# A two-layer hybrid encoder trunk on one core: loads in order of need, block 1 transposed behind the first unit, zero products, and the last two units of a segment finished one PSUM bank ahead of the other

## The chip, the cores and the metric

The kernel runs on one core of one Trainium2 chip. The metric is device time in microseconds (us) of one execution; the figure for a kernel is the median of its runs.

## The reference

A sequence of 256 frames of width 1024 goes through two layers. Each layer computes, with ALPHA = (2*2)^(1/4):

```python
x = layer_norm(ALPHA * x + 0.5 * swiglu(x, ffn1_w_gu[l], ffn1_w_down[l]), ln1_g[l], ln1_b[l])
h = x @ w_in[l]                      # one input projection for three groups of heads
...                                  # differential attention | Mamba-2 SSD | gated DeltaNet
x = layer_norm(ALPHA * x + mix, ln2_g[l], ln2_b[l])      # mix = concat(heads) @ w_out[l]
x = layer_norm(ALPHA * x + 0.5 * swiglu(x, ffn2_w_gu[l], ffn2_w_down[l]), ln3_g[l], ln3_b[l])
```

`swiglu(x, gu, down)` is `(silu(gate) * up) @ down` with `gate, up` the two halves of `x @ gu`; the inner width is 2816. Everything is float32. The change touches only how the big products are fed and ordered, not the heads between `w_in` and `w_out`.

## The kernel before

**Blocks and segments.** The 256 frames are two blocks of 128 rows, b = 0 and b = 1, held in the tiles `x0` and `x1` (the order listings below call them `x_91` and `x_92`). The work is six segments: FFN 1, mix and FFN 2 of layer 0, then of layer 1. At a segment's end each block is normalised (`norm`: `x` plus the segment's output, mean and variance, gain and bias) and transposed (`make_xT`), and the next segment starts from the transposed tiles `xT`, one for each half of the 1024 columns. So there are five boundaries between segments: 0 to 1 and 3 to 4 go from FFN 1 into mix, 2 to 3 from FFN 2 into FFN 1, and 1 to 2 and 4 to 5 from mix into FFN 2.

**Units.** A segment is a list of units. A unit is one piece of weights of at most 1024 columns per partition: loaded by SP's DMA queue into a tile `raw` (`load`, 5 buffers), then split by ACT and DVE into a high part `wh` and a low part `wl` (`split`, 7 buffers each, two halves per unit). Float32 accuracy comes from three products of split operands (`mm3`, lines 217 to 228): high times high, high times low, low times high. Line 221 is xh*wh, line 222 xh*wl, lines 224 and 228 xl*wh; line 228 stands after both banks, line 224 is used on a unit that ends its sum:

```python
for p, (wh, wl) in zip(ps, ws):
    mm(p, lhsT=xh, rhs=wh, ...)          # 221
    mm(p, lhsT=xh, rhs=wl, ...)          # 222
    if stop: mm(p, lhsT=xl, rhs=wh, ...) # 224
if not stop:
    for p, (wh, wl) in zip(ps, ws): mm(p, lhsT=xl, rhs=wh, ...)  # 228
```

So a product with `xl` needs DVE's subtraction at line 233 (`xT<-xps,xT`), a product with `xh` only ACT's copy at line 232. The first two column groups of an FFN and some units of mix run one block at a time; the others ("both") run both blocks in one pass with the weights stationary (line 301). The `down` and `w_out` units at a segment's end run one block at a time into two PSUM banks `po[0]` and `po[1]`, one for each half of the output's columns.

**Which block runs when.** `order` (line 1107) lists (block, unit) pairs. In a segment's first and last phase block 0 runs ahead of block 1 by up to LAG = 5 units. At the end block 0 finishes its last unit five units before block 1 does, so block 0's norm and its transposition can run beside block 1's remaining products.

**What sets the order on the engines.** The Python program emits instructions while it advances a clock of its own (`self.clock`) by the length of each product; `norm`, `make_xT` and the like are generators that yield a number of microseconds and are taken up again by `step` once that clock has passed (`spawn`, `go`, `step`). `norm` yields 5.5 (times 0.9) before it goes on to `make_xT` (line 389). The tile framework then assigns the emitted instructions to the engines' queues; every engine works through its queue strictly in order. `norm` reads `po[0]` at its first line-375 instruction and `po[1]` at its second, takes statistics (376, 378), an inverse root on POOL (394, 396) and writes `x` in halves (382, 383).

**The start.** `setup` loads 64 KB of constants and `x0` in two halves of 256 KB, `prepare` loads five units (two DMAs of 256 KB each), then `x1` follows. `make_xT` is spawned for both blocks before the first product. In segment 0 units 0 to 3 hold the first column group, units 0 and 1 for the first half of the 1024 inputs, units 2 and 3 for the second.

Of the kernel before, what the change touches and what calls it, by code (L numbers as in the profile page):

```python
# [17 lines left out]
P = 128  # L18
# [5 lines left out]
NCH = DFF // 256  # L24
# [67 lines left out]
class Kernel:  # L92
# [47 lines left out]
    def setup(self):  # L140
        nc, a = self.nc, self.a
        c = self.const
        self.x = [c.tile([P, D], F32, name=f"x{b}") for b in range(2)]
        cst = c.tile([P, C_N], F32, name="cst")
        nc.sync.dma_start(cst[:, 0:P], a["cst"][:, 0:P])
        self.load_x(0)
        self.cst = cst
        self.ident = cst[:, C_ID : C_ID + P]
        self.UT = cst[:, C_UT : C_UT + P]
        self.SL = cst[:, C_SL : C_SL + P]  # L150
        self.M1 = cst[:, C_M1 : C_M1 + 64]
        self.ident64 = cst[:, C_I64 : C_I64 + 64]
        self.sel = cst[:, C_SEL : C_SEL + 2]
        self.neghalf = c.tile([P, 16], F32, name="neghalf")
        nc.gpsimd.memset(self.neghalf, -0.5)

    def load_x(self, b):
        for n in range(2):
            s = slice(n * 512, (n + 1) * 512)
            self.nc.sync.dma_start(self.x[b][:, s], self.a["x"][0, b * P : (b + 1) * P, s])  # L160

    def setup_late(self):

# [77 lines left out]
    def load(self, u):  # L241
        nc = self.nc
        raw = self.raw_p.tile([P, 1024], F32, tag="raw", name=self.name("raw"))
        if u["kind"] in ("gu", "win"):
            width, ks = u["width"], u["ks"]
            t = raw[:, : ks * width].rearrange("p (k n) -> p k n", k=ks)
            at = 0
            k0 = u["part"] * ks * P
            for c0, n in u["cols"]:
                nc.sync.dma_start(  # L250
                    t[:, :, at : at + n], u["w"][k0 : k0 + ks * P, c0 : c0 + n].rearrange("(k p) n -> p k n", p=P)
                )
                at += n
            u["n"] = ks * width
        else:
            nc.sync.dma_start(raw, u["w"][u["k"] * P : (u["k"] + 1) * P, :])
            u["n"] = 1024
        u["raw"] = raw
# [16 lines left out]
    def job(self, u, b):  # L275


        wh, wl = u["wh"], u["wl"]
        if u["kind"] in ("gu", "win"):
            width, ks = u["width"], u["ks"]  # L280
            g = u["group"]
            if u["part"] == 0:
                g["ps", b] = [self.ps("ps") for _ in range(2 if u["kind"] == "gu" and u["both"] else 1)]
            banks = g["ps", b]
            last = u["part"] == KD // ks - 1
            if u["both"]:
                for i, c0 in enumerate(u["tiles"]):
                    for kk in range(ks):
                        k = u["part"] * ks + kk
                        x = self.xT[k // 4][:, k % 4].rearrange("p a b t -> p a (b t)")  # L290
                        s = slice(kk * width + c0, kk * width + c0 + P)
                        end = last and kk == ks - 1
                        if len(banks) == 2:

                            o, first = banks[i][:, 0:256], k == 0
                            mms = [(banks[i], wh[:, s], x.rearrange("p a t -> p (a t)")), (o, wl[:, s], x[:, 0])]
                        else:
                            o, first = banks[0][:, 256 * i : 256 * i + 256], k == 0 and i == 0
# [12 lines left out]
            ps = banks[0][:, :width]  # L311
            for kk in range(ks):
                k = u["part"] * ks + kk
                xh, xl = (self.xT[k // 4][:, k % 4, part, b, :] for part in range(2))
                s = slice(kk * width, (kk + 1) * width)
                self.mm3([ps], xh, xl, [(wh[:, s], wl[:, s])], k == 0, k == KD - 1)
            if last:
                self.spawn(u["then"](u, b, ps))
        else:
            if u["first"]:  # L320
                self.po[b] = [self.ps("po") for _ in range(2)]
            parts = self.hT if u["kind"] == "down" else self.mT
            t, kk = parts[u["k"] // 2, b], u["k"] % 2
            ws = [(wh[:, n * 512 : (n + 1) * 512], wl[:, n * 512 : (n + 1) * 512]) for n in range(2)]
            po = self.po[b]
            self.mm3(po, t[:, 0, kk, :], t[:, 1, kk, :], ws, u["first"], u["last"])
            if kk == 1:
                del parts[u["k"] // 2, b]
            if u["last"]:
                self.spawn(u["then"](u, b, po))  # L330
# [68 lines left out]
    def make_xT(self, b, seg):  # L399


        x = self.x[b]
        if b == 0:
            self.next_xT = []
        for n in range(2):
            ps = self.aux(b, "xps")
            self.transposes([x[:, (4 * n + k) * P : (4 * n + k + 1) * P] for k in range(4)], ps)
            if b == 0:
                self.next_xT.append(self.xt_p.tile([P, 4, 2, 2, P], F32R, tag="xt", name=self.name("xT")))
            t = self.next_xT[n]  # L410
            self.split_from(ps.rearrange("p (k t) -> p k t", k=4), t[:, :, 0, b], t[:, :, 1, b])
            yield 0.7
            self.xT = self.next_xT
            self.xready.add((seg, n, b))

    def to_parts(self, t, b, src, name):

# [629 lines left out]
    def segments(self):  # L1047
        a = self.a
        segs = []

        def ffn(l, f):
            seg = len(segs)
            last = l == L - 1 and f == 2
            units = []
# [15 lines left out]
                        )  # L1070
            for k in range(2 * NCH):
                units.append(
                    dict(kind="down", w=a[f"ffn{f}_w_down"][l], k=k, first=k == 0, last=k == 2 * NCH - 1, both=False,
                         then=lambda u, b, po: self.norm(b, po, 0.5, seg, last))
                )
            n = 1 if f == 1 else 3
            segs.append((units, (a[f"ln{n}_g"][l], a[f"ln{n}_b"][l])))

        def mix(l):
# [10 lines left out]
                    )  # L1090
            for n, k in enumerate(WORD):
                units.append(
                    dict(kind="wout", w=a["w_out"][l], k=k, first=n == 0, last=n == 7, both=False,
                         then=lambda u, b, po: self.norm(b, po, 1.0, seg, False))
                )
            segs.append((units, (a["ln2_g"][l], a["ln2_b"][l])))
# [3 lines left out]
            mix(l)  # L1100
            ffn(l, 2)
        for n, (units, _) in enumerate(segs):
            for u in units:
                u["seg"] = n
        return segs

    def order(self, units):


        n = len(units)  # L1110
# [13 lines left out]
        closing = lambda at, hi: min(LAG, max(1, LAG - (hi - at[0]) // 2))  # L1124
        if first is None:
            first = stop
        phase(0, first, opening)
        out.extend((None, i, 0) for i in range(first, stop))
        phase(stop, n, closing)
        return out  # L1130

    def run(self):
        self.chains = []
        self.clock = 0.0
        self.hT, self.mT, self.mx, self.po, self.xready = {}, {}, {}, [None, None], set()
        self.ahead = NW
# [14 lines left out]
        def products(u, b):  # L1151
            while not ("wh" in u and self.ready(u, b)):
                prepare()
                if self.chains:
                    self.clock = max(self.clock, min(c[0] for c in self.chains))
                    self.step()
            self.job(u, b)
            if b != 0:
                count["done"] += 1
            prepare()  # L1160
            self.step()

        prepare()
        self.load_x(1)
        prepare()
        for b in range(2):
            self.spawn(self.make_xT(b, 0))
        for n, (seg, gb) in enumerate(segs):
            self.mx.clear()
            for m, (b, i, lag) in enumerate(self.order(seg)):  # L1170

                self.ahead = max(NW - 2, lag + 2) if seg[-1]["kind"] == "wout" else NW
                products(seg[i], b)
                if m == 4 * LAG:
                    self.load_gb(*gb)
                    if n == 0:
                        self.spawn(self.setup_late())
# [39 lines left out]
```

## Time and profile before

| | |
|---|---|
| median of 3 runs | 1095.92 us (1094.84 to 1097.18) |
| profiled execution, own time | 1094.49 us |
| its span | 1092.7 us |
| PE busy | 1052.6 us, 96% of the span |
| DVE busy | 759.1 us, 69% |
| ACT busy | 600.2 us, 55% |
| moved by DMA | 184.99 MB, mean 169 GB/s |

The profile is of one execution. A line of its timeline gives a start and a length in microseconds from the span's start, the engine, the line of the code, the operation, what it writes and reads, how many of a kind were merged (x4), and in brackets how long the engine had sat idle before it and who ended that. PE is TensorE's products, PEld its weight loads, SPq the queue that issues DMAs. Products overlap, so the distance from one start to the next, not the length, is what a product costs.

### The profile page before, as it was taken

The numbers are of one execution on the slowest core, as the hardware profiler recorded it, in microseconds if no ns is written. First come the engines' busy times: TensorE is split into PE (matmuls) and PEld (weight loads), VectorE is DVE, ScalarE is ACT, GpSimd is POOL, SyncE is SP. The second block draws the span as 40 slices with busy tenths as digits, with TensorE's granted clock in tenths as the row PEclk, the third lists the DMA queues.
The fourth block names the chain that finished last, engine by engine and source line by source line (L and its number), as shares of the span: only waits on it lengthen the run. The fifth ranks groups of instructions, "written<-read, shape, count | busy, mean of one in ns | idle before, by whom it ended". The sixth has DMA issues, their size and how long they took to land.

```text
span 1092.7 us, 17702 instructions
## 1 busy us (share of the span) xinstructions
PE 1052.6 (96%) x6397; PEld 896.7 (82%) x6397; DVE 759.1 (69%) x1531; ACT 600.2 (55%) x1284; POOL 42.0 (4%) x51
## 2 busy tenths in 40 slices
PE   6999999999998999999999999999989999999996
PEld 5888878788887788888878888877878877888885
DVE  5767754886867877774587776467967688777644
ACT  6677643487543566664346665436764345666530
POOL 0000000001001100000000000000010110000001
PEclk9999999999999999999999999999999999999999
DMA  9977665661234776666477666637513258666641
GB/s 289 255 210 203 197 195 144 174 193 40 72 104 140 206 214 193 191 188 196 139 225 207 188 193 191 193 98 206 161 40 98 89 159 245 185 192 193 194 134 39
DMA packets 222351, 184.99 MB, mean 169 GB/s; under 512 B 15160, under 2 KB 201912, under 8 KB 222264
## 3 DMA queue, kind: packets, MB, share of 16 engines
q1 hardware_dynamic: 222264, 183.87, 56.9%
q8 instruction: 50, 0.82, 0.3%
q14 instruction: 37, 0.30, 0.1%
HBM read 182.78 MB, written 1.05 MB: 168 GB/s over the span
## 4 chain that ended last, share of the span: by engine, by line
PE 79%; DVE 11%; ACT 3%; DMA 3%; issue 2%; POOL 2%; SPq 0%; DVEq 0%; POOLq 0%; ACTq 0%
PE ps L301 39%; PE po L221 7%; PE po L222 7%; PE po L228 7%; DVE wl L233 4%; PE ps L221 4%; PE ps L222 4%; PE ps L228 3%; DMA raw<-in_ffn_w_gu_dram 2%; PE ups L355 1%; PE gps L355 1%; DMA raw<-in_w_in_dram 1%; ACT wh L232 1%; POOL rsq L396 1%; PE vnps L355 1%
## 5 line engine op out<-in xcount | busy, mean ns | idle before, releaser
L233 DVE TENSOR_TENSOR wl<-raw,wh 128x512 fp32r<-128x512 f32 (+1 forms) x672 | 437.8, 682 | 191.9 <-ACT wh L232 185.3
L232 ACT CAST wh<-raw 128x512 fp32r<-128x512 f32 (+1 forms) x672 | 386.5, 615 | 205.8 <-PE po L228 99.7
L301 PE MATMUL ps<-xT,wh 128*128 128x512 f32 (+1 forms) x1600 | 484.8, 363 | 0.0
L301 PE MATMUL ps<-xT,wl 128*128 128x256 f32 x1376 | 388.4, 282 | 0.0
L301 PEld LDWEIGHTS ps<-xT,wh 128*128 128x128 f32 x1600 | 285.3, 188 | 48.6 <-issue 1.1
L301 PEld LDWEIGHTS ps<-xT,wl 128*128 128x128 f32 x1376 | 260.5, 189 | 0.7 <-issue 0.5
L221 PE MATMUL po<-wh,hT 128*128 128x512 f32 x352 | 137.7, 391 | 0.8 <-DVE hh L457 0.8
L222 PE MATMUL po<-wl,hT 128*128 128x512 f32 x352 | 137.1, 389 | 0.0
L228 PE MATMUL po<-wh,hT 128*128 128x512 f32 x336 | 103.5, 389 | 0.0
L221 PE MATMUL ps<-wh,xT 128*128 128x512 f32 (+2 forms) x256 | 97.1, 379 | 4.3 <-ACT wh L232 4.2
L222 PE MATMUL ps<-wl,xT 128*128 128x512 f32 (+2 forms) x256 | 94.6, 371 | 0.0
L228 PE MATMUL ps<-wh,xT 128*128 128x512 f32 (+2 forms) x224 | 83.6, 374 | 3.4 <-DVE xT L233 3.4
L221 PEld LDWEIGHTS po<-wh,hT 128*128 128x128 f32 x352 | 66.1, 188 | 15.7 <-DVE hh L457 2.2
L222 PEld LDWEIGHTS po<-wl,hT 128*128 128x128 f32 x352 | 66.1, 188 | 13.4
L228 PEld LDWEIGHTS po<-wh,hT 128*128 128x128 f32 x336 | 63.1, 188 | 13.2
L232 ACT CAST hT<-hh 128x256 fp32r<-128x256 f32 x72 | 29.2, 406 | 71.9 <-DVE hh L459 71.9
L221 PEld LDWEIGHTS ps<-wh,xT 128*128 128x128 f32 x256 | 48.5, 190 | 13.6 <-ACT wh L232 5.0
L222 PEld LDWEIGHTS ps<-wl,xT 128*128 128x128 f32 x256 | 48.6, 190 | 8.3 <-DVE wl L233 0.6
L458 ACT ACTIVATE ga<-ga 128x256 f32<-128x256 f32 x72 | 30.1, 418 | 42.4 <-DVE ga L455 42.2
L228 PEld LDWEIGHTS ps<-wh,xT 128*128 128x128 f32 x224 | 42.4, 189 | 11.1 <-DVE xT L233 4.2
L233 DVE TENSOR_TENSOR hT<-hh,hT 128x256 fp32r<-128x256 f32 x72 | 30.5, 424 | 25.8 <-ACT hT L232 25.6
L394 POOL TENSOR_SCALAR rs<-mv 128x1 f32<-128x1 f32 x12 | 6.3, 526 | 790.9 <-DVE mv L378 790.9
(233 smaller groups left out, 970.9 us busy)
## 6 DMA issues: line engine op xcount, KB each, us to landing
raw<-in_ffn_w_gu_dram SPq DMA_DIRECT2D x352, 256.0 KB, 3.5
raw<-in_ffn_w_down_dram SPq DMA_DIRECT2D x88, 512.0 KB, 3.5
raw<-in_w_in_dram SPq DMA_DIRECT2D x40, 512.0 KB, 3.8
raw<-in_w_out_dram SPq DMA_DIRECT2D x16, 512.0 KB, 3.5
raw<-in_w_in_dram SPq DMA_DIRECT2D x24, 256.0 KB, 3.9
g<-in_ln_g_dram SPq DMA_DIRECT2D x6, 512.0 KB, 5.5
b<-in_ln_b_dram SPq DMA_DIRECT2D x6, 512.0 KB, 5.6
x<-in_x_dram SPq DMA_DIRECT2D x4, 256.0 KB, 3.4
```

Source lines behind the costliest of these rows:

```text
L221: mm(p, lhsT=xh, rhs=wh, start=start, stop=False)
L222: mm(p, lhsT=xh, rhs=wl, start=False, stop=False)
L228: mm(p, lhsT=xl, rhs=wh, start=False, stop=False)
L232: self.nc.scalar.copy(hi, src)
L233: self.nc.vector.tensor_tensor(lo, src, hi.bitcast(F32), op=ALU.subtract)
L301: self.nc.tensor.matmul(to, lhsT=a, rhs=r, start=first and n == 0, stop=end and n == len(mms) - 1, skip_group_check=True,)
L355: self.nc.tensor.matmul(out, lhsT=lhsT, rhs=rhs, start=start, stop=stop)
L394: nc.gpsimd.tensor_scalar(t, ap, mul, add, op0=ALU.mult, op1=ALU.add)
L396: nc.gpsimd.tensor_tensor(r, t, self.neghalf[:, :n], op=ALU.pow)
L458: nc.scalar.activation(a, a, AF.Silu)
```

## The change

Five edits, in the start and at the ends of segments.

- **Loads.** `load_x` loads one half of one block. The order on SP's queue is now: constants, first half of `x0`, unit 0, first half of `x1`, unit 1, second half of `x0`, second half of `x1`, unit 2 and so on. Unit 0 (`begin`) is loaded in four DMAs of 128 KB, one k-slice at a time, instead of two of 256 KB.
- **Transposition.** `make_xT` of block 1 is spawned behind the first unit; in segment 0 a half counts as ready as soon as it is emitted, and `make_xT` waits 5 (times 0.9) between the halves. `order` runs segment 0's first phase with a lag of 1 unit, so both blocks use a unit one behind the other.
- **Zero products.** A tile of zeros, six 128x128 products of it before the first transposition and four behind it.
- **Banks.** The last two units of `down` and `w_out` are `late`: the products of the first of them into bank 1 are held back, bank 0 takes both units and is finished, then bank 1 takes both.
- **Bookkeeping.** While products are held, `done` is not counted up; the last unit counts 2.

```diff
-        self.load_x(0)
+        self.load_x(0, 0)
...
+        self.zero = self.h(0, [P], "zero")
+        nc.vector.memset(self.zero, 0.0)
+
+    def idle_products(self, n):
+        ps = self.aux(0, "idle")
+        for _ in range(n):
+            self.nc.tensor.matmul(ps[:, 0:P], lhsT=self.zero, rhs=self.zero, start=True, stop=True)
...
-            at = 0
             k0 = u["part"] * ks * P
-            for c0, n in u["cols"]:
...
+            step = 1 if u["begin"] else ks
+            for k in range(0, ks, step):
...
-            self.mm3(po, t[:, 0, kk, :], t[:, 1, kk, :], ws, u["first"], u["last"])
+            if u["late"] and not u["last"]:
+
+                self.mm3(po[:1], t[:, 0, kk, :], t[:, 1, kk, :], ws[:1], False, False)
+                self.held[b].append((t[:, 0, kk, :], t[:, 1, kk, :], ws[1:]))
+            elif u["last"]:
+                self.mm3(po[:1], t[:, 0, kk, :], t[:, 1, kk, :], ws[:1], False, True)
+                for xh, xl, w in self.held[b]:
+                    self.mm3(po[1:], xh, xl, w, False, False)
+                self.held[b] = []
+                self.mm3(po[1:], t[:, 0, kk, :], t[:, 1, kk, :], ws[1:], False, True)
+            else:
+                self.mm3(po, t[:, 0, kk, :], t[:, 1, kk, :], ws, u["first"], False)
...
-            yield 0.7
+            if seg:
+                yield 0.7
             self.xT = self.next_xT
             self.xready.add((seg, n, b))
+            if not seg:
+                yield 5
...
-                    dict(kind="down", w=a[f"ffn{f}_w_down"][l], k=k, first=k == 0, last=k == 2 * NCH - 1, both=False,
+                    dict(kind="down", w=a[f"ffn{f}_w_down"][l], k=k, first=k == 0, last=k == 2 * NCH - 1, late=k >= 2 * NCH - 2, both=False,
...
-        phase(0, first, opening)
+        phase(0, first, (lambda at, hi: 1) if start else opening)
...
-            if b != 0:
-                count["done"] += 1
+            if b != 0 and not self.held[1]:
+                count["done"] += 2 if u.get("last") else 1
...
-        prepare()
-        self.load_x(1)
-        prepare()
+        self.idle_products(6)
+        self.load(units[0])
+        self.load_x(1, 0)
+        self.load(units[1])
         for b in range(2):
-            self.spawn(self.make_xT(b, 0))
+            self.load_x(b, 1)
+        count["load"] = 2
+        self.spawn(self.make_xT(0, 0))
+        self.idle_products(4)
...
+                if n == m == 0:
+                    self.spawn(self.make_xT(1, 0))
```

What this does to the queues, at three places. Numbers behind a name tell buffers apart; line numbers of the changed kernel are higher (221 becomes 228, 228 becomes 235, 233 becomes 240, 237 becomes 244, 375 to 383 become 396 to 404).

TensorE at the start, before: the last products of unit 1, the first of unit 4 (`wh_201`), then the transpositions of `x1` first half, `x0` second half, `x1` second half (`xps`).

```order
L228 MATMUL ps_164<-wh_140,xT_130 128x512
L221 MATMUL ps_164<-wh_140,xT_130 128x512
L222 MATMUL ps_164<-wl_141,xT_130 128x512
L228 MATMUL ps_164<-wh_140,xT_130 128x512
L221 MATMUL ps_229<-wh_201,xT_130 128x512
L237 MATMUL xps_133<-cst,x_92 128x128 x4
L237 MATMUL xps_149<-cst,x_91 128x128 x4
L237 MATMUL xps_157<-cst,x_92 128x128 x4
```

TensorE at the start, now, from its first product: the zero products, the first half of `x0`, unit 0 (`wh_131`), the first product of unit 1 (`wh_164`).

```order
L163 MATMUL idle_100<-zero_98 128x128 x6
L244 MATMUL xps_118<-cst,x_91 128x128 x4
L163 MATMUL idle_126<-zero_98 128x128 x4
L228 MATMUL ps_157<-wh_131,xT_123 128x512
L229 MATMUL ps_157<-wl_132,xT_123 128x512
L235 MATMUL ps_157<-wh_131,xT_123 128x512
L228 MATMUL ps_157<-wh_131,xT_123 128x512
L229 MATMUL ps_157<-wl_132,xT_123 128x512
L235 MATMUL ps_157<-wh_131,xT_123 128x512
L228 MATMUL ps_157<-wh_164,xT_123 128x512
L244 MATMUL xps_149<-cst,x_91 128x128 x4
L244 MATMUL xps_173<-cst,x_92 128x128 x4
```

The transpositions of `x0`'s second and `x1`'s first half now stand behind seven products instead of thirteen, with no product of a fifth unit ahead of them.

VectorE at the boundary from segment 0 to 1, before: `wl` are low halves of the next segment's weights, `po_1616` and `po_1617` the two banks of block 1, `xT_2069` and `xT_2107` the low parts of block 0's transposed halves.

```order
L233 TENSOR_TENSOR wl_2041<-raw_1916,wh_2040 128x272 x2
L233 TENSOR_TENSOR wl_2056<-raw_1944,wh_2055 128x272 x2
L233 TENSOR_TENSOR xT_2069<-xps_2064,xT_2069 128x4x128
L375 SCALAR_TENSOR_TENSOR x_92<-po_1616,x_92 128x512
L375 SCALAR_TENSOR_TENSOR x_92<-po_1617,x_92 128x512
L376 BN_STATS stats_2078<-x_92 128x6 x2
L233 TENSOR_TENSOR wl_2094<-raw_1972,wh_2093 128x272
L378 BN_AGGR mv_2083<-stats_2078 128x2
L233 TENSOR_TENSOR wl_2094<-raw_1972,wh_2093 128x272
L382 SCALAR_TENSOR_TENSOR x_92<-x_92,mv_2083,g_571 128x512 x2
L383 SCALAR_TENSOR_TENSOR x_92<-x_92,rsq_2087,b_572 128x512 x2
L233 TENSOR_TENSOR xT_2107<-xps_2102,xT_2107 128x4x128
```

VectorE at the same boundary now: `po_1632` and `po_1633` are block 1's banks, `xT_2106` and `xT_2114` block 0's transposed halves.

```order
L240 TENSOR_TENSOR wl_2042<-raw_1906,wh_2041 128x512 x2
L240 TENSOR_TENSOR wl_2057<-raw_1932,wh_2056 128x272 x2
L396 SCALAR_TENSOR_TENSOR x_92<-po_1632,x_92 128x512
L396 SCALAR_TENSOR_TENSOR x_92<-po_1633,x_92 128x512
L397 BN_STATS stats_2077<-x_92 128x6 x2
L240 TENSOR_TENSOR wl_2093<-raw_1960,wh_2092 128x272
L399 BN_AGGR mv_2082<-stats_2077 128x2
L240 TENSOR_TENSOR wl_2093<-raw_1960,wh_2092 128x272
L403 SCALAR_TENSOR_TENSOR x_92<-x_92,mv_2082,g_587 128x512 x2
L404 SCALAR_TENSOR_TENSOR x_92<-x_92,rsq_2086,b_588 128x512 x2
L240 TENSOR_TENSOR xT_2106<-xps_2101,xT_2106 128x4x128
L240 TENSOR_TENSOR xT_2114<-xps_2109,xT_2114 128x4x128
```

Block 0's low part `xT`, which stood ahead of block 1's norm, now stands behind the whole of it.

TensorE at the same boundary, before: block 1's last unit (`wh_1910`) between the two transpositions of block 0, then the next segment's products.

```order
L228 MATMUL po_1617<-wh_1884,hT_1529 128x512
L237 MATMUL xps_2064<-cst,x_91 128x128 x4
L221 MATMUL po_1616<-wh_1910,hT_1529 128x512
L222 MATMUL po_1616<-wl_1911,hT_1529 128x512
L224 MATMUL po_1616<-wh_1910,hT_1529 128x512
L221 MATMUL po_1617<-wh_1910,hT_1529 128x512
L222 MATMUL po_1617<-wl_1911,hT_1529 128x512
L224 MATMUL po_1617<-wh_1910,hT_1529 128x512
L237 MATMUL xps_2102<-cst,x_91 128x128 x4
L221 MATMUL ps_2110<-wh_1938,xT_2069 128x512
L222 MATMUL ps_2110<-wl_1939,xT_2069 128x512
L221 MATMUL ps_2150<-wh_2040,xT_2069 128x272
```

TensorE there now: the end of block 1's bank 1, then block 0's transpositions, four products, then block 1's transpositions (`x_92`).

```order
L228 MATMUL po_1633<-wh_1926,hT_1545 128x512
L229 MATMUL po_1633<-wl_1927,hT_1545 128x512
L231 MATMUL po_1633<-wh_1926,hT_1545 128x512
L244 MATMUL xps_2101<-cst,x_91 128x128 x4
L244 MATMUL xps_2109<-cst,x_91 128x128 x4
L228 MATMUL ps_2117<-wh_1954,xT_2106 128x512
L229 MATMUL ps_2117<-wl_1955,xT_2106 128x512
L228 MATMUL ps_2164<-wh_2056,xT_2106 128x272
L229 MATMUL ps_2164<-wl_2057,xT_2106 128x272
L244 MATMUL xps_2136<-cst,x_92 128x128 x4
L244 MATMUL xps_2157<-cst,x_92 128x128 x2
L235 MATMUL ps_2117<-wh_1954,xT_2106 128x512
```

All of block 0's transpositions moved behind block 1's last product, and block 1's moved ahead of the first product that needs a low part (line 235), from behind 28 products of the new segment to behind four.

More of the change, by code (lines that the diff above doesn't have):

```diff
@@ L155, in setup, with load_x @@
         nc.gpsimd.memset(self.neghalf, -0.5)
[L157 to L160, printed above, removed]
+        self.zero = self.h(0, [P], "zero")
[4 more added lines that the diff above has]
+            self.nc.tensor.matmul(ps[:, 0:P], lhsT=self.zero, rhs=self.zero, start=True, stop=True)
+    def load_x(self, b, n):
+        s = slice(n * 512, (n + 1) * 512)
+        self.nc.sync.dma_start(self.x[b][:, s], self.a["x"][0, b * P : (b + 1) * P, s])
     def setup_late(self):
@@ L246, in load @@
             t = raw[:, : ks * width].rearrange("p (k n) -> p k n", k=ks)
-            at = 0
             k0 = u["part"] * ks * P
-            for c0, n in u["cols"]:
[L250 to L253, printed above, removed]
+            step = 1 if u["begin"] else ks
+            for k in range(0, ks, step):
+                at = 0
+                r = slice(k0 + k * P, k0 + (k + step) * P)
+                for c0, n in u["cols"]:
+                    nc.sync.dma_start(
+                        t[:, k : k + step, at : at + n], u["w"][r, c0 : c0 + n].rearrange("(k p) n -> p k n", p=P)
+                    )
+                    at += n
             u["n"] = ks * width
@@ L1092, in mix @@
                 units.append(
-                    dict(kind="wout", w=a["w_out"][l], k=k, first=n == 0, last=n == 7, both=False,
+                    dict(kind="wout", w=a["w_out"][l], k=k, first=n == 0, last=n == 7, late=n >= 6, both=False,
                          then=lambda u, b, po: self.norm(b, po, 1.0, seg, False))
@@ L1102, in segments, with order @@
         for n, (units, _) in enumerate(segs):
-            for u in units:
+            for m, u in enumerate(units):
                 u["seg"] = n
+                u["begin"] = n == 0 and m == 0
         return segs
-    def order(self, units):
+    def order(self, units, start):
         n = len(units)
@@ L1132, in run @@
     def run(self):
-        self.chains = []
+        self.chains, self.held = [], [[], []]
         self.clock = 0.0
@@ L1157, in products @@
             self.job(u, b)
-            if b != 0:
-                count["done"] += 1
+            if b != 0 and not self.held[1]:
+                count["done"] += 2 if u.get("last") else 1
             prepare()
             self.step()
-        prepare()
-        self.load_x(1)
-        prepare()
+        self.idle_products(6)
+        self.load(units[0])
+        self.load_x(1, 0)
+        self.load(units[1])
         for b in range(2):
-            self.spawn(self.make_xT(b, 0))
+            self.load_x(b, 1)
+        count["load"] = 2
+        self.spawn(self.make_xT(0, 0))
+        self.idle_products(4)
         for n, (seg, gb) in enumerate(segs):
             self.mx.clear()
-            for m, (b, i, lag) in enumerate(self.order(seg)):
+            for m, (b, i, lag) in enumerate(self.order(seg, n == 0)):
                 self.ahead = max(NW - 2, lag + 2) if seg[-1]["kind"] == "wout" else NW
                 products(seg[i], b)
+                if n == m == 0:
+                    self.spawn(self.make_xT(1, 0))
                 if m == 4 * LAG:
```

## Prediction, made before the run

> **What bounds the kernel now.** I read the page's shares first, then its slices.
>
> ```profile
> span 1092.7 us, 17702 instructions
> PE 1052.6 (96%) x6397; PEld 896.7 (82%) x6397; DVE 759.1 (69%) x1531; ACT 600.2 (55%) x1284; POOL 42.0 (4%) x51
> PE   6999999999998999999999999999989999999996
> ```
>
> TensorE (PE) is busy 96% of the span and in nearly every slice; it is the bound, and an edit is worth the PE idle time that it takes away or adds. What PE waited for, by waits (total, times, longest):
>
> ```profile
> PE xps L237 <- DMA x<-in_x_dram: 4.6, 1, 4.6
> PE xps L237 <- DVE x L383: 3.4, 4, 1.1
> PE ps L228 <- DVE xT L233: 3.4, 3, 1.6
> ```
>
> The first is the start, the last two the boundaries between segments, where block 1's norm (L383) and block 0's low part (L233) are awaited. The change touches just these places, and the tail.
>
> The timeline of the start, PE and the casts that feed it:
>
> ```profile
> 4.56 1.09 PE L237 MATMUL xps<-cst,x 128*128 128x128 f32 x4 [4.56 <-DMA x<-in_x_dram]
> 5.69 0.58 ACT L232 CAST xT<-xps 128x512 fp32r<-128x512 f32 x1 [3.69 <-PE xps L237]
> 8.66 0.79 PE L221 MATMUL ps<-wh,xT 128*128 128x512 f32 x1 [3.02 <-ACT wh L232]
> 9.45 1.14 ACT L232 CAST wh<-raw 128x512 fp32r<-128x512 f32 x2 [0.31 <-DMA raw<-in_ffn_w_gu_dram]
> ...
> 10.41 0.63 PE L221 MATMUL ps<-wh,xT 128*128 128x512 f32 x1
> 10.84 0.63 PE L222 MATMUL ps<-wl,xT 128*128 128x512 f32 x1
> 12.12 0.41 PE L222 MATMUL ps<-wl,xT 128*128 128x512 f32 x1
> 12.36 0.40 PE L228 MATMUL ps<-wh,xT 128*128 128x512 f32 x1
> 14.95 1.47 PE L237 MATMUL xps<-cst,x 128*128 128x128 f32 x12
> 17.06 0.40 PE L222 MATMUL ps<-wl,xT 128*128 128x512 f32 x1
> ```
>
> From start to start a product costs 0.43 us at 10.41 and 0.23 from 12.12 on. PE is dense only from 14.95 on, with twelve transpositions first.
>
> The first boundary (segment 0 to 1):
>
> ```profile
> 196.18 0.60 PE L237 MATMUL xps<-cst,x 128*128 128x128 f32 x4
> 196.21 3.30 DVE L233 TENSOR_TENSOR wl<-raw,wh 128x512 fp32r<-128x512 f32 x7
> 196.53 0.47 PE L221 MATMUL po<-wh,hT 128*128 128x512 f32 x1
> 198.00 0.60 PE L237 MATMUL xps<-cst,x 128*128 128x128 f32 x4
> 199.42 0.69 DVE L233 TENSOR_TENSOR xT<-xps,xT 128x512 fp32r<-128x512 f32 x1
> 200.02 1.28 DVE L375 SCALAR_TENSOR_TENSOR x<-po,x 128x512 f32<-128x512 f32 x2
> 200.16 0.50 PE L228 MATMUL ps<-wh,xT 128*128 128x512 f32 x1 [0.85 <-DVE xT L233]
> 205.31 1.32 PE L237 MATMUL xps<-cst,x 128*128 128x128 f32 x8 [0.64 <-DVE x L383]
> 205.83 2.15 DVE L233 TENSOR_TENSOR xT<-xps,xT 128x512 fp32r<-128x512 f32 x3
> ```
>
> Block 1's last product is issued by 198.00. Its norm on DVE runs from 200.02, and its transpositions follow at 205.31: a chain of 5.29 us. Beside it PE works on block 0's new segment, since block 0's low part (199.42) comes ahead of the chain. PE loses 0.85 + 0.64, and inside the eight transpositions, which cost 0.35 us per four (196.18 to 196.53) and took 1.32, another 0.62: 2.1 us.
>
> **The start: a gain of 3.5 us.** Loading unit 0 behind half of `x0` instead of all of it saves one DMA of 256 KB; unit 1 has the same bytes ahead of it as before (cst, two halves of x, unit 0), so its cast starts near 9.45 again. Unit 0's cast started at 8.00 before:
>
> ```profile
> 8.00 1.14 ACT L232 CAST wh<-raw 128x512 fp32r<-128x512 f32 x2 [1.72 <-DMA raw<-in_ffn_w_gu_dram]
> ```
>
> The first 128 KB pair should let it start when ACT is through with xT, 6.3 (5.69 + 0.58), first product some 7.0 to 7.4 (the zero products behind the transposition may hold it). Six products of unit 0 end before unit 1's first cast half is ready at 10.0. Then by the order: one product, eight transpositions (0.7), ACT's and DVE's halves of two xT tiles (0.58 and 0.69 each, behind unit 1's split, which ends near 11.4), so block 1's low part at 12.8, and by then seven more products. PE is dense from about 13.0 with 14 products and 13 transpositions done, 14 x 0.23 + 13 x 0.09 = 4.4 us of work: 8.6 lost. Before, at 17.06, it had done 15 and 16, 4.9 us: 12.2 lost. Gain 3.6, less slack: 3.5. Bounds: if PE stays at 0.43 until unit 1, its transpositions and products come 1.3 later: 2.2; at best PE never waits behind unit 1's arrival: 4. The zero products and the memset run before data is there and cost nothing; behind the transposition four at 0.43 end at 7.4, in the estimate above.
>
> **The tail: a gain of 0.6.**
>
> ```profile
> 1083.01 1.37 DVE L375 SCALAR_TENSOR_TENSOR x<-po,x 128x512 f32<-128x512 f32 x2 [0.69 <-PE po L224]
> 1083.26 0.39 PE L224 MATMUL po<-wh,hT 128*128 128x512 f32 x1
> 1084.30 1.27 DVE L376 BATCH_NORM_STATS2 stats<-x 128x6 f32<-128x512 f32 x2
> ```
>
> Bank 0 ends six products (1.36 us) ahead of bank 1, not three. DVE is idle there, and the order is now add, statistics, add, statistics: one statistics, half of 1.27, moves ahead of the last product.
>
> **The boundaries: a loss of 12.8.** Here the early bank buys nothing, because DVE isn't free: at block 1's last product (198.00) it is still in seven subtractions that end at 199.42. What decides is a side effect. The unit held back adds only half a unit to the program's clock; the 5.5 x 0.9 = 4.95 us that block 0's norm yields pass after four whole units of 1.28 (5.1) before, but three and a half are 4.5, so now `make_xT` of block 0 is taken up behind block 1's last unit, whose norm is emitted first. The order shows it: on DVE block 0's low part stands behind the whole norm of block 1; on PE block 1's transpositions stand behind four products, and the next needs that low part.
>
> Segment 0 to 1, in the trace's own times: block 1's last product issued by 197.65 (four transpositions, 0.35, left its path). Block 1's norm starts at 200.02 - 0.60 (xT gone from ahead of it) - 0.70 (two of the seven subtractions gone, of width 272) = 198.7. Its transpositions: + 5.29 = 204.0. Block 0's low part follows 0.52 later (205.83 - 205.31) and takes 0.69: PE goes on at 205.25. In these 7.6 us it has 14 transpositions (1.2) and four products, two of them short (0.7): 5.7 idle, against 2.1. Loss 3.6; I take 3.5. Segment 3 to 4 has the same order: 3.5.
>
> ```profile
> 545.64 4.30 DVE L233 TENSOR_TENSOR wl<-raw,wh 128x512 fp32r<-128x512 f32 x7
> 547.42 0.60 PE L237 MATMUL xps<-cst,x 128*128 128x128 f32 x4
> 550.46 1.28 DVE L375 SCALAR_TENSOR_TENSOR x<-po,x 128x512 f32<-128x512 f32 x2
> 550.60 0.49 PE L228 MATMUL ps<-wh,xT 128*128 128x512 f32 x1 [1.65 <-DVE xT L233]
> 550.93 0.39 PE L221 MATMUL ps<-wh,xT 128*128 128x512 f32 x1
> 551.16 0.39 PE L222 MATMUL ps<-wl,xT 128*128 128x512 f32 x1
> 556.24 1.32 PE L237 MATMUL xps<-cst,x 128*128 128x128 f32 x8
> ```
>
> Segment 2 to 3: last product by 547.07; norm from 550.46 - 0.60 - 2 x 0.60 = 548.66; chain 5.78 (550.46 to 556.24): 554.44; low part + 1.2: 555.7. Of 8.6 us 2.1 are work: 6.5 idle against 1.65 + 0.62. Loss 4.2.
>
> ```profile
> 359.26 1.89 DVE L233 TENSOR_TENSOR wl<-raw,wh 128x512 fp32r<-128x512 f32 x3
> 361.03 0.60 PE L237 MATMUL xps<-cst,x 128*128 128x128 f32 x4
> 367.54 1.29 PE L237 MATMUL xps<-cst,x 128*128 128x128 f32 x8 [1.07 <-DVE x L383]
> ```
>
> Behind mix (1 to 2, 4 to 5) DVE's order puts block 0's low part behind two adds, two statistics and three subtractions, not the whole norm. From 359.26 eight steps of 0.6 (a subtraction ahead of them too) and 0.7: 364.8 at the latest, 364.1 if DVE keeps its pace of before, against a last product at 360.68. PE has 1.4 us of work there: some 2.4 idle with what follows, against 1.07 + 0.59. Loss 0.8 each, 1.6 for two (0.4 to 3).
>
> Sum of the boundaries: 3.5 + 3.5 + 4.2 + 1.6 = 12.8. Net: 12.8 - 3.5 - 0.6 = +8.7. The profiled execution took 1094.49 (span 1092.7 and 1.8 around it), so 1103.2; it lies 1.4 below the median, to which I add the same: 1095.92 + 8.7 = **1104.6**. Elsewhere the order shifts a little inside mix, with no instruction gained; I allow 2 either way. Two runs of this kernel can be told apart from about 0.2% (2.2 us).
>
> **The rivals.**
>
> *The clock falls in the new stalls.* PE would stand still for about 4.1 us (two boundaries; 199.9 to 204.0) and 4.9 us (one). The trace shows no such stall inside: after 1.65 idle products still cost 0.23 (550.93 to 551.16). At the start, after 3.02 idle, eight products took 8.66 to 12.12, 3.46, instead of 1.8. If each long stall costs that 1.65, it is 3 x 1.65 = 5 more: 1109.6. The Trainium skill (TensorE: Matmul & The Clock Gate, "What's actually happening") says that the clock halves after an idle window of about 3.4 us, windows that run on their own, and recovers after a busy one; by that rule a stall just over a window halves it in some cases. The trace's 3.46 us at the slow pace agrees with its length; that a stall brings it back no row here shows. Chance 0.22.
>
> *Early banks pull the norm forward: faster.* If DVE came to bank 0 when it is done, 1.36 us ahead of the last product, each boundary would save some 0.68 and its stall would not grow: 1095.92 - 3.5 - 0.6 - 5 x 0.68 = 1088.4. It decides at DVE's backlog: it would have to end by about 196.5 where the rows show 199.42, and block 0's xT would have to stay off the path, against the order. Chance 0.07.
>
> *The stalls are half absorbed.* PE loses them, but the chains inside mix, which PE waits for later, catch up meanwhile: 12.8 becomes 6 to 9, 1098 to 1101. Mix holds idle spells of 1.5 us at most, so little can be given back. Chance 0.12.
>
> *The start doesn't do what it says* (zero products don't raise the clock early): gain 2.2, 1105.9, inside the forecast.
>
> Chances: forecast (1101 to 1107.5) 0.55, clock 0.22, absorbed 0.12, faster 0.07, no change 0.04. The range 1099 to 1111 leaves out the faster case, no change and the ends of the others.
>
> **What would show it.** Right: PE's first product near 7, dense from 13; at three boundaries a PE wait of over 4 us on `x` (line 404), then a short one on `xT` (line 240), and DVE's add of block 1 ahead of block 0's `xT`; last products within 8.6 us of the end. The clock rival shows as a pitch of 0.43 behind the stalls. Wrong: waits at the boundaries no longer than before, or dense PE at the start as late as 16.

## The result, and the profile after

The changed kernel takes 1107.02 us (median of four runs, 1106.22 to 1108.91), the kernel before 1095.38 beside it: a ratio of 1.0103, 95% interval 1.0089 to 1.0118. It is slower by 11.6 us; 1104.6 was forecast, in a range of 1099 to 1111. The profiled execution is 11.7 longer (span 1104.4 against 1092.7), and what follows here is read from it. Two executions far outside the rest, 1492.84 us of kept_one_load and 2097.66 of start_only2, are left out of the figures below.

The page of the changed kernel:

```profile
span 1104.4 us, 17745 instructions
PE 1063.8 (96%) x6417; PEld 906.7 (82%) x6417; DVE 758.8 (69%) x1532; ACT 601.7 (54%) x1284; POOL 41.3 (4%) x51
PEclk9999999999999999999989999998999999999998
```

PE is "busy" 11.2 us longer. Some 4.6 of that are its 20 new matmul instructions, all of them short zero products (1.03 to 3.96 and 4.91 to 6.61). The rest hints that the lost time isn't idle time alone: a product that runs at half the clock counts as busy for longer (0.63 us instead of 0.40 in the rows below). Two of the three dips in the row of the granted clock, in the slices that begin at 552 and 745 us, stand just past places where segments meet; the third is the end of the span. Behind the first boundary the granted clock is 0.50 from 200.8 to 204.2 us, too short to show in that row.

What PE waited for, in total, number and longest:

```profile
PE xps L244 <- DVE x L404: 12.5, 3, 4.5
...
PE ps L235 <- DVE xT L240: 1.8, 2, 0.9
PE ps L228 <- ACT wh L239: 1.3, 1, 1.3
```

Three waits for block 1's norm (L404) hold 12.5 us; before, the four waits for it held 3.4. The wait of 4.6 for the first transfer has gone from the list, since zero products now fill the time ahead of it, and one of 1.3 for unit 1's cast is what the start has left.

The start of the changed kernel:

```profile
6.37 0.48 PE L228 MATMUL ps<-wh,xT 128*128 128x512 f32 x1
...
9.89 0.51 PE L228 MATMUL ps<-wh,xT 128*128 128x512 f32 x1 [1.34 <-ACT wh L239]
10.47 1.10 PE L244 MATMUL xps<-cst,x 128*128 128x128 f32 x8
...
13.10 0.27 PE L244 MATMUL xps<-cst,x 128*128 128x128 f32 x1
```

Six products from 6.37 on, a wait until unit 1's cast at 9.89, then the eight transpositions, and PE is dense with 14 products done by 13.1, as the sum had it.

The first boundary (segment 0 to 1), PE and DVE:

```profile
193.83 0.40 PE L231 MATMUL po<-wh,hT 128*128 128x512 f32 x1
194.06 1.03 PE L244 MATMUL xps<-cst,x 128*128 128x128 f32 x8
195.24 1.28 DVE L396 SCALAR_TENSOR_TENSOR x<-po,x 128x512 f32<-128x512 f32 x2
195.53 0.50 PE L228 MATMUL ps<-wh,xT 128*128 128x512 f32 x1 [0.44 <-ACT xT L239]
...
196.24 0.29 PE L229 MATMUL ps<-wl,xT 128*128 128x272 f32 x1
...
200.52 1.35 PE L244 MATMUL xps<-cst,x 128*128 128x128 f32 x6 [3.99 <-DVE x L404]
201.04 1.88 DVE L240 TENSOR_TENSOR xT<-xps,xT 128x512 fp32r<-128x512 f32 x3
201.78 0.80 PE L235 MATMUL ps<-wh,xT 128*128 128x512 f32 x1
202.38 0.63 PE L228 MATMUL ps<-wh,xT 128*128 128x512 f32 x1
202.80 0.63 PE L229 MATMUL ps<-wl,xT 128*128 128x512 f32 x1
...
204.63 0.40 PE L228 MATMUL ps<-wh,xT 128*128 128x512 f32 x1
```

Block 1's last product is at 193.83. PE has four products for block 0, then nothing until block 1's norm is through on DVE, 195.24 to 200.52: a chain of 5.28 us, 5.29 before. It is not longer; it used to run beside PE's work, and now PE stands in front of it, since block 0's low parts (201.04) come behind it. And when PE goes on, products start 0.42 apart (202.38 to 202.80); only at 204.63 is it 0.23 again.

**Where the 11.7 us are.** One landmark per segment, block 1's last product, tells it. Two of them in the kernel before, at the ends of segments 0 and 3:

```profile
197.76 0.40 PE L224 MATMUL po<-wh,hT 128*128 128x512 f32 x1
...
734.32 0.40 PE L224 MATMUL po<-wh,hT 128*128 128x512 f32 x1
```

All of them, in us of the profiled executions:

| segment | last product before | after | length before | after | added |
|---|---|---|---|---|---|
| 0 | 197.76 | 193.83 | | | -3.6 (start) |
| 1 (mix) | 360.80 | 360.99 | 163.04 | 167.16 | +4.1 |
| 2 | 547.18 | 547.75 | 186.38 | 186.76 | +0.4 |
| 3 | 734.32 | 741.60 | 187.14 | 193.85 | +6.7 |
| 4 (mix) | 897.35 | 908.85 | 163.03 | 167.25 | +4.2 |
| 5 | 1083.26 | 1095.61 | 185.91 | 186.76 | +0.5 |
| tail, to the end | | | 9.44 | 8.79 | -0.65 |

Segments 0 and 5 are corrected by 0.35, for four transpositions that stood ahead of that product before and stand behind it now. The five segments behind the boundaries add 15.9; with start and tail that is 11.7, the whole difference.

Not all of the 15.9 is the boundaries'. In segment 3 the 576 products with the weights stationary (line 311) take 101.86 us from the first to the last, 100.02 in the kernel before and in segments 2 and 5 of this same trace. The 1.8 us are spread evenly (from 600 to 620 us PE takes 115 products where the kernel before takes 118) and the granted clock is 1.00 there. Other traces have the same step in other segments, clock_kept for one in 2 and 3, with no long stall ahead; late_only and warm_stall have it nowhere. What causes it isn't known. It is called the slower pass below. Without it the boundaries add 14.1.

### The profile page after: what moved, and what is told of

It reads as the page before. It is cut to its first block, busy times and chain, and to the rows that moved or that the text cites. A ratio compares the mean times of both kernels' runs of the same rounds, so it can differ in the third digit from the quotient of the medians.

```text
span 1104.4 us, 17745 instructions
## 1 busy us (share of the span) xinstructions
PE 1063.8 (96%) x6417; PEld 906.7 (82%) x6417; DVE 758.8 (69%) x1532; ACT 601.7 (54%) x1284; POOL 41.3 (4%) x51
## 4 chain that ended last, share of the span: by engine, by line
PE 82%; DVE 9%; ACT 3%; POOL 2%; DMA 2%; issue 1%; SPq 1%; POOLq 0%; DVEq 0%; ACTq 0%
PE ps L311 41%; PE po L228 7%; PE po L229 7%; PE po L235 7%; PE ps L229 4%; PE ps L228 4%; PE ps L235 4%; DVE wl L240 2%; PE ups L376 1%; PE gps L376 1%; ACT wh L239 1%; POOL rsq L417 1%; DVE x L404 1%; PE xps L244 1%; PE vnps L376 1%
## 5 line engine op out<-in xcount | busy, mean ns | idle before, releaser
L240 DVE TENSOR_TENSOR wl<-raw,wh 128x512 fp32r<-128x512 f32 (+1 forms) x672 | 438.9, 682 | 197.0 <-ACT wh L239 189.4
L311 PE MATMUL ps<-xT,wh 128*128 128x512 f32 (+1 forms) x1600 | 492.9, 367 | 0.0
L228 PE MATMUL ps<-wh,xT 128*128 128x512 f32 (+2 forms) x256 | 97.9, 383 | 4.3 <-ACT xT L239 3.0
L235 PE MATMUL ps<-wh,xT 128*128 128x512 f32 (+2 forms) x224 | 85.6, 383 | 1.8 <-DVE xT L240 1.8
L228 PEld LDWEIGHTS ps<-wh,xT 128*128 128x128 f32 x256 | 49.3, 192 | 13.9 <-ACT xT L239 4.6
L481 DVE TENSOR_TENSOR hh<-ps,hh 128x256 f32<-128x256 f32 x72 | 30.2, 419 | 9.2 <-ACT hh L480 9.2
```

Source lines behind the costliest of these rows:

```text
L228: mm(p, lhsT=xh, rhs=wh, start=start, stop=False)
L235: mm(p, lhsT=xl, rhs=wh, start=False, stop=False)
L240: self.nc.vector.tensor_tensor(lo, src, hi.bitcast(F32), op=ALU.subtract)
L311: self.nc.tensor.matmul(to, lhsT=a, rhs=r, start=first and n == 0, stop=end and n == len(mms) - 1, skip_group_check=True,)
L481: nc.vector.tensor_add(hh, up[:, 0:256], hh)
```

## The experiments

Two theories were on trial. **Order**: the loss comes from the moment at which block 0's transpositions are taken up, which the held unit shifts by counting half. **Banks**: the early bank makes the loss by itself. Beside them stood the question how much of the loss is standing still and how much is the lower clock afterwards.

**clock_kept** restores the program's clock alone:

```diff
                 self.held[b].append((t[:, 0, kk, :], t[:, 1, kk, :], ws[1:]))
+                self.clock += 3 * 512 / 2400
...
                     self.mm3(po[1:], xh, xl, w, False, False)
+                    self.clock -= 3 * 512 / 2400
```

> The changed kernel, but the held unit moves the program's clock on by its full 1.28 us (0.64 of it taken back when its second half is issued), so that block 0's transpositions are taken up where they stood before; products, banks and waits on data stay those of the change. Theory (order): the three stalls of 4 us and what follows them go away, 1107.0 - 15.9 of the boundaries, start and tail keep their 3.6 and 0.65: about 1091, between 1089 and 1093. Rival (the early bank itself, by weights that stay in use longer and a bank that ends later): the boundaries keep most of their loss, 1102 or more.

Measured: 1086.43 us (1084.31 to 1089.88), a ratio of 0.993 to the kernel before (0.9915 to 0.9945). Its waits for block 1's norm:

```profile
PE xps L244 <- DVE x L406: 1.5, 2, 0.8
```

Its first boundary, where block 0's low part goes through DVE ahead of block 1's add again and PE works through the norm:

```profile
196.94 0.68 DVE L240 TENSOR_TENSOR xT<-xps,xT 128x512 fp32r<-128x512 f32 x1
...
197.54 1.27 DVE L398 SCALAR_TENSOR_TENSOR x<-po,x 128x512 f32<-128x512 f32 x2
197.67 0.50 PE L235 MATMUL ps<-wh,xT 128*128 128x512 f32 x1
...
202.82 1.32 PE L244 MATMUL xps<-cst,x 128*128 128x128 f32 x8 [0.76 <-DVE x L406]
```

Some 20 us below the changed kernel, by two lines that touch only the program's own clock, and so only the order. It came out 2.6 us below the expected range, which counted no gain at the boundaries beyond undoing the loss. (The profiled execution, 1089.88 us, holds the slower pass twice.)

**yield_49** gets at the same moment from the other side, in the changed kernel:

```diff
-            yield 5.5
+            yield 4.9
```

> The changed kernel with one number moved: the norm yields 4.9 instead of 5.5 ahead of its transpositions (4.9 x 0.9 = 4.41 us of the program's clock, under the 4.5 that three and a half units make). Theory: the transpositions are taken up where clock_kept takes them up, so the time is that of clock_kept, 1084 to 1088. Rival (in clock_kept something else than the moment of taking up helped): over 1095.

Measured: 1088.11 us (1085.80 to 1089.33), ratio 0.9937 (0.9918 to 0.9955), at the upper edge of what was expected (1088) and 19 us below the changed kernel.

**before_62** does the reverse: it makes the loss in the kernel before, with none of the change in it.

```diff
-            yield 5.5
+            yield 6.2
```

> The kernel before, with nothing of the change, and one number moved: the norm yields 6.2 instead of 5.5 before it goes on to its transpositions, so that at all five boundaries block 0's are taken up behind block 1's last unit. Theory (it is the moment of taking up, not the early banks): the three boundaries between FFN segments lose what they lost in the changed kernel, 15, and the two behind mix a stall of the same kind, 3.5 to 5 each: 1094.6 + 22 to 25 = 1117 to 1120. Rival (the held units make the loss): 1094 to 1097.

Measured: 1125.65 us (1123.62 to 1127.55), ratio 1.0271 (1.0251 to 1.0292). The direction and the place are those of the theory, the size is some 6 us above its range. Its waits:

```profile
PE xps L237 <- DVE x L383: 19.5, 5, 5.6
```

Five waits for block 1's norm, where the changed kernel has three: the boundaries behind mix join in, with two waits each (1.25 for `wl` and 2.25 for `x` at the first), and products at half pace behind them. By the same landmarks each of the five segments is longer, by 4.9 to 6.8 us; segments 2 and 5 hold the slower pass, 3.7 us together, as much as this execution lies above the range (1123.62 against 1120). So the late taking-up makes the loss without any early bank. The three runs together settle that it is the moment of taking up.

**late_only** has the held units without the new start (the diff is the change's, less the start).

> The kernel before with the held units alone: no zero products, loads and start as before. Theory: all of the boundaries' loss and the tail's gain, 1095.4 + 15.9 - 0.65 = 1110.7. Rival (the loss needs the new start, whose lead meets a late DVE): 1096 to 1100.

Measured: 1109.47 us (1107.56 to 1112.38), ratio 1.0138 (1.0124 to 1.0152). Its waits for block 1's norm are those of the changed kernel:

```profile
PE xps L237 <- DVE x L394: 12.6, 3, 4.6
```

The loss doesn't need the new start, and the two parts add up: 1107.0 with the start is 2.5 less, and the start alone gains 2.1 (start_only2 below).

**start_only** was to be the other half; `late` is false for all units.

> The changed kernel with no unit held back (every unit ends both banks together, as before); start, loads and zero products stay. Theory: the start is worth 3.6 us and nothing else is left, 1095.4 - 3.6 = 1091.8. Rival (the start's lead is eaten by the first boundary, since DVE is the late one there): about 1095.

Measured: 1105.11 us (1102.05 to 1105.89), ratio 1.0088. Neither of the two. The kernel was at fault, not the start: the change counts two units as done at the last one of a segment, and with no unit held back that counts one too many each time, so the splitting of weights ran further ahead with each segment. The loss shows in its segments: against start_only2, segment 1 is 2.3 us longer, and segments 3, 4 and 5 are 3 to 4 each. It says nothing about the start, but how dear splits are that are issued too early: 12 us against start_only2, of which 1.8 is the slower pass in segment 3 of the profiled execution.

**start_only2** mends that:

```diff
-                count["done"] += 2 if u.get("last") else 1
+                count["done"] += 1
```

> The start alone once more, with no unit held back, and now with one unit counted as done per unit (in start_only the last unit of a segment was still counted twice, so that splits ran further ahead from segment to segment). Theory: the start is worth 3.6 us and touches nothing else, 1094.6 - 3.6 = 1091.0. If the miscount was not what made start_only slow, it stays near 1105; if the start's lead is eaten at the first boundary, 1094.

Measured: 1093.27 us (1091.12 to 1096.41), ratio 0.9979 (0.9967 to 0.9992): a gain of 2.1 us, less than the 3.6 expected. In its profile block 1's last product in segment 0 stands at 194.06 against 197.76, so the start itself gave 3.7; 1.1 of it was lost again by the last segment's end, most of it in the two mix segments, and why isn't settled (the medians of these kernels move by 1 to 2 us). Against clock_kept the held units, with the moment of taking up put right, are worth 1093.3 - 1086.4 = 6.9 us, tail included. That this is the early bank's doing isn't shown. At the first boundary of kept_no_zero (below), which holds the units as clock_kept does, DVE adds both banks of block 1 in one go, 1.5 us behind the start of its last product (194.44 to 195.95), in start_only2 2.25 behind it (194.06 to 196.31). What differs ahead of that is the order: five subtractions instead of seven stand before block 0's low part, and its first transposition stands eight products ahead of block 1's last instead of six.

**warm_stall** asks how much is the clock. It lets PE multiply what it has, into a bank that nobody reads, while it waits:

```diff
+FILL = {1: 15, 3: 17, 4: 15}
...
+        elif seg in FILL:
+            idle = self.aux(1, "idle").rearrange("p (k t) -> p k t", k=4)
+            xh = self.next_xT[1][:, :, 0, 0]
+            for _ in range(FILL[seg]):
+                self.nc.tensor.matmul(idle, lhsT=xh[:, 0], rhs=xh, start=True, stop=True)
```

> The changed kernel with 15, 17 and 15 idle products of 128x512 put into the three long stalls (their results go to a bank that nobody reads). The waits for block 1's norm stay. Theory (clock): the 22 products behind the stalls that took 0.43 us go back to 0.23, 4.4 us, and the transpositions among them some 0.5: 1102 (1101 to 1103.5). Rival (the slow pace hides behind DVE's late low parts, so that it costs nothing): 1106 to 1107.5.

Measured: 1100.43 us (1099.84 to 1100.90), ratio 1.0053 (1.004 to 1.0066), 0.6 below the expected range. The place of segment 2 to 3, first in the changed kernel:

```profile
555.44 1.54 PE L244 MATMUL xps<-cst,x 128*128 128x128 f32 x6 [4.54 <-DVE x L404]
...
557.30 0.63 PE L228 MATMUL ps<-wh,xT 128*128 128x512 f32 x1
557.73 0.63 PE L229 MATMUL ps<-wl,xT 128*128 128x512 f32 x1
```

and in warm_stall:

```profile
549.83 4.10 PE L431 MATMUL idle<-xT 128*128 128x512 f32 x17
554.55 1.38 PE L245 MATMUL xps<-cst,x 128*128 128x128 f32 x8 [0.62 <-DVE x L405]
...
556.22 0.40 PE L236 MATMUL ps<-wh,xT 128*128 128x512 f32 x1
556.45 0.39 PE L229 MATMUL ps<-wh,xT 128*128 128x512 f32 x1
```

The norm's data come no sooner (7.7 us behind block 1's last product, 546.85 here and 547.75 there), but the products behind them start 0.23 apart instead of 0.43. The median falls by 6.6 us, or by 5.8 if each is taken against the kernel before that ran beside it (1095.38 and 1094.55); 5 was expected. By the landmarks segment 3 is 3.1 shorter than in the changed kernel, segments 1 and 4 are 1.3 and 1.4 shorter, 5.8 in all. But 1.8 of the 3.1 is the slower pass, which this execution doesn't have. So the clock behind the three stalls accounts for 4.0, some 1.3 each. The run also moved one or two products across the transpositions, so a few tenths may be order. What segments 1 to 5 are still longer than in the kernel before, 10.0 together, is left to standing still.

**warm_half** leaves part of each stall idle (8 products in each).

> warm_stall (1100.4) with only 8 idle products in each of the three long stalls, so that 2.2, 2.9 and 2.2 us of each stay idle. If the clock falls only behind a stall of about 3.4 us without a break, as the Trainium skill's rule has it: 1100 to 1101, no slow products. If shorter stalls do it too (behind a wait of 2.6 us in start_only seven products took 0.43): some of the three boundaries pay 1.3 to 3 again, 1102 to 1105.

Measured: 1104.91 us (1103.52 to 1106.64), ratio 1.0088 (1.0069 to 1.0108). Two of its boundaries, 0 to 1 and then 2 to 3:

```profile
203.32 1.38 PE L245 MATMUL xps<-cst,x 128*128 128x128 f32 x8 [2.19 <-DVE x L405]
...
205.23 0.40 PE L229 MATMUL ps<-wh,xT 128*128 128x512 f32 x1
205.46 0.40 PE L230 MATMUL ps<-wl,xT 128*128 128x512 f32 x1
```

```profile
556.95 1.84 PE L245 MATMUL xps<-cst,x 128*128 128x128 f32 x8 [2.65 <-DVE x L405]
...
559.46 0.63 PE L229 MATMUL ps<-wh,xT 128*128 128x512 f32 x1
559.88 0.63 PE L230 MATMUL ps<-wl,xT 128*128 128x512 f32 x1
```

Behind 2.19 idle the pace held, behind 2.65 it fell. So a stall need not last 3.4 us without a break. Segment 3 was as long as in the changed kernel (193.7 us, 190.8 in warm_stall), but 1.8 of those 3.0 us is the slower pass again; the fall of the clock took 1.1. In this execution the start was slow as well (five products at 0.43 between 12.0 and 13.9; block 1's last product of segment 0 stands 2.3 us later than in warm_stall). So that the time fits the second expectation is largely luck: the boundaries have 1.1 of the 5.2 us by which this execution is longer.

**kept_no_zero** is clock_kept without its zero products.

> clock_kept (1086.4) without its ten zero products. Theory (they raise the clock early): unit 0's six products take 0.43 instead of 0.23, and the slow pace lasts into unit 1's, 1.5 to 2 us: 1088. Rival (PE waits for unit 1's cast at 9.9 in any case, and six slow products from 6.4 end at 9.0): no change, 1086 to 1087.

Measured: 1086.25 us (1083.34 to 1091.16), ratio 0.9918 (0.9895 to 0.9941), within 0.2 of clock_kept and as the rival had it. Its start:

```profile
6.16 0.79 PE L228 MATMUL ps<-wh,xT 128*128 128x512 f32 x1 [1.19 <-ACT wh L239]
...
8.92 0.63 PE L235 MATMUL ps<-wh,xT 128*128 128x512 f32 x1
10.28 0.50 PE L228 MATMUL ps<-wh,xT 128*128 128x512 f32 x1 [0.73 <-ACT wh L239]
...
11.73 0.39 PE L235 MATMUL ps<-wh,xT 128*128 128x512 f32 x1
11.96 0.40 PE L228 MATMUL ps<-wh,xT 128*128 128x512 f32 x1
```

Unit 0's six products do take 0.43 and more each, but the wait for unit 1's cast covers it, and by then the pace is 0.23 (11.73 to 11.96) without any zero product. The zero products change the pace and not the time, as far as the scatter of these runs lets one see.

**kept_one_load** is clock_kept with unit 0 in two transfers (`step = ks`).

> clock_kept (1086.4) with unit 0 loaded in two transfers of 256 KB again instead of four of 128 KB. Theory: its cast starts some 0.7 us later, but its products still end before unit 1's cast is there, so no change beyond 0.5: 1086 to 1087. Rival (every stage of the start moves with the first cast): 1087 to 1088.

Measured: 1084.01 us (1083.31 to 1085.81), ratio 0.9894 (0.9876 to 0.9913), 2 us below the expected range. The four smaller transfers bring nothing either. Whether two are better by the 2.4 us to clock_kept isn't shown: the intervals of the two ratios all but touch (0.9913 and 0.9915), and those of this run and kept_no_zero overlap. What the start gained is left to the order of the loads and of the transpositions, which no run separates.

**kept_early** goes on from there: kept_one_load, with the norm's yield at 4.0.

> kept_one_load (1084.5) with the norm's yield at 4.0, so that both of block 0's transpositions stand eight products ahead of block 1's last and its low parts go through DVE before block 1's norm. Theory: block 1's norm starts up to 0.6 us earlier and the waits of 0.75 and 0.4 us that are left at three boundaries shrink: 1083 to 1084.5. Rival (block 0's norm isn't through by then, and PE waits for x0 instead, some 0.8 us at each of five boundaries): 1087 to 1089.

Measured: 1082.39 us (1081.22 to 1084.91), ratio 0.9884 (0.9862 to 0.9906). It came out 0.6 below the expected range. No wait for block 1's norm is left in it; the longest ones of PE lie inside mix:

```profile
PE mTps L244 <- DVE go L762: 3.4, 2, 1.7
PE mTps L244 <- DVE d L560: 2.9, 2, 1.5
```

It beats both kernels, by 1.2% the one before and by 2.2% the changed one (1082.39 against 1107.02). The 1.6 us to kept_one_load are not clear of noise: the intervals of the two ratios overlap.

## Why the prediction was right, and where it wasn't

**The boundaries' mechanism: right, and shown.** The held unit counts half, `make_xT` of block 0 misses its moment, and its low parts end up behind block 1's norm. Keeping the count cures it, moving one number cures it, and the other way round one number makes it in the kernel before.

**Their size: near, in part by luck.** 12.8 was forecast; 14.1 came, and 1.8 more of the slower pass, which nobody foresaw. Two errors offset each other. Standing still was priced too high: 3.5, 4.2 and 3.5 at the three long stalls, where the segments of warm_stall are 2.8, 3.6 and 2.8 longer than before, and 0.8 twice behind mix against 0.3 and 0.4; why isn't shown. And the sentence on which the likeliest case rested, that an edit is worth the PE idle time that it adds, failed: the clock fell behind each of the three stalls. The rival that said so, at a chance of 0.22, put it at 5 us and 1109.6; warm_stall puts it at 4.0. The measured 1107.02 lies halfway between the two cases. The rival should have been the likeliest case: the only argument against it was that the trace of before held no such stall, and the start of that same trace did show the slow pace behind 3.02 us of idle. The granted clock of the kernel before also stands at 0.50 from 264.7 to 268.1 us, inside mix.

The Trainium skill (TensorE: Matmul & The Clock Gate, "What's actually happening") has the clock halve after an idle window of about 3.4 us, and that agrees in outcome here with stalls of 4.0 to 4.5. Read as the length of one wait it doesn't agree with the 2.65 us in warm_half; the last section has more on this.

**"Here the early bank buys nothing": right.** At the first boundary DVE begins block 1's add at 195.24, 1.4 us behind the start of the last product, and takes both banks in one go. Behind mix the first bank is added early, at 360.49 against a last product at 360.99, but the segment is 0.4 longer all the same. With the moment put right the held units do gain, 6.9 us against start_only2, but not as the rival "early banks pull the norm forward" had it. That needed DVE free 1.3 us ahead of block 1's last product; in clock_kept it is in subtractions until 1 us behind it (197.0 and 196.03). That the rival's price, 1088.4, is near the 1086.4 and 1088.1 of clock_kept and yield_49 is luck.

**The start: right in time, wrong in one cause.** 3.6 against 3.5, dense at 13.1 against 13.0. But the bound that gave 1.3 us to the clock at the start was empty: kept_no_zero is as fast without zero products.

**The tail:** 0.65 against 0.6, one statistics ahead of the last product (1095.41 and 1095.61 in these rows of the changed kernel):

```profile
1095.41 0.69 DVE L397 BATCH_NORM_STATS2 stats<-x 128x6 f32<-128x512 f32 x1
1095.61 0.39 PE L231 MATMUL po<-wh,hT 128*128 128x512 f32 x1
1096.04 0.69 DVE L396 SCALAR_TENSOR_TENSOR x<-po,x 128x512 f32<-128x512 f32 x1
```

**"The stalls are half absorbed": no.** The landmark of segment 4 still has the whole of segment 3's loss and 4.2 more.

## What to carry to other kernels

Where a program decides by its own estimate of time when a chain goes on, an edit that only splits or holds work also moves that estimate: look in the order of the engines for what now stands behind a whole norm, before asking what the edit saves. A new stall on TensorE is to be priced with the slow products behind it, some 1.3 us apiece here. And an idea that lost by a side effect deserves one run with the side effect undone; here that turned +1.0% into -0.7%.

## What was not expected of the hardware

The slow pace can come late, and behind short stalls. In start_only PE was back at work behind a wait of 2.57 us and ran 1.5 us at full pace before it fell:

```profile
551.34 0.50 PE L235 MATMUL ps<-wh,xT 128*128 128x512 f32 x1 [2.57 <-DVE xT L240]
551.67 0.40 PE L228 MATMUL ps<-wh,xT 128*128 128x512 f32 x1
...
553.30 0.63 PE L228 MATMUL ps<-wh,xT 128*128 128x512 f32 x1
553.73 0.63 PE L229 MATMUL ps<-wl,xT 128*128 128x512 f32 x1
```

In late_only it fell behind two waits of 0.72 and 0.89 us with three products between them, for eight products. It held behind 2.19 us in warm_half and behind 1.65 in the kernel before. Once fallen, the granted clock stood at half for 3.4 or 6.8 us.

The same section of the Trainium skill says that the windows run on by themselves, so that the point at which the clock changes depends on where in one the first product falls. The traces agree as to the windows: in each of the thirteen, all changes of the granted clock lie a whole number of 3.41 us apart. What ends in a fall is such a stretch of 3.4 us in which PE was mostly idle, whatever the length of a single wait. PE was busy for 0.28 us of it at the first boundary of the changed kernel (197.4 to 200.8), 0.75 ahead of the fall in warm_half (553.9 to 557.3), 1.36 in start_only (549.3 to 552.7) and 1.79 in late_only (909.0 to 912.4). The wait of 2.19 in warm_half fell across two stretches, with 2.23 and 2.28 busy, and the clock held. In start_only the stretch ended 1.5 us after PE had gone back to work, hence the late fall. Up to the end of the last segment, all 31 stretches that began at the full clock and had PE busy for less than 45% ended in a fall. Above that the limit isn't sharp: before held at 1.75 us (548.0 to 551.4), late_only fell at 1.79. Six falls inside mix follow a stretch of short products in which PE counts as busy throughout, and this doesn't explain them.

The slower pass was not expected either. The pass of 576 products takes either 100.0 or 101.8 to 101.9 us at a granted clock of 1.00, in 10 of the 39 FFN segments behind the first that these traces hold. One such pass makes an execution 1.8 us longer, and why a pass is the slow one stays open.
